# Index keys gathered by depth, without transposes, and a buffer of their own for block B's keys

## The chip, the cores and the metric

The kernel runs on one core of a Trainium2 chip. The metric is the device time of one execution in microseconds (us), as the median of several runs. A profiled execution gives the rows below.

## The reference

One step of a hybrid layer: RMSNorm, one combined input projection, sparse attention beside a gated short convolution, and an output projection. 1024 prompt rows and 8 sequences of 4 new tokens each go through it.

```python
p = split_proj(rmsnorm(x, norm_in) @ w_in)          # q, k, v, z_attn, q_idx, k_idx, w_idx, h, b, c, z_conv
...
dots = jnp.einsum("bthd,bld->bthl", qi, ki)          # 16 index heads of 64
s = jnp.einsum("bth,bthl->btl", wi, jax.nn.relu(dots))
_, idx = lax.top_k(s, 256)                           # the keys that attention may use
...
ki_past = cache_kidx[page_table].reshape(Bd, past, IDX_DIM)   # decode: 8 x 8192 cached index keys of 64
...
return x + mix @ w_out
```

## The kernel before, in words

The activations are kept transposed, as 16 chunks of 128 columns of the model width, each as a high and a low part (`xh`, `xl`). A weight tile is loaded as 128x4x128 (`w`, SyncE's queue), split by ScalarE into a high part `wh` and by VectorE into a low part `wl` (`load_w`, L485), and TensorE multiplies three products of the parts into `pj` (`proj`, L498). `wh` and `wl` have three buffers each, so a tile's `wl` can't be written before TensorE has read the one three tiles earlier. The weight tiles are numbered here in the order in which TensorE meets them, from 1; a tile of block B is 12 `pj` matmuls of 512 columns.

Block A is the first 512 prompt rows with the 32 decode rows, block B the other 512 prompt rows. After every tile `slot()` lets four pipes go on by a unit: index scores and attention of the prompt, the decode sequences' scores, selection and attention, and others. All of it is in one program, and the order on each engine is fixed when the program is built; an engine runs its rows strictly in that order.

The decode index is 64 units `keys(g, s)` (L1092), one for each group of 1024 cached keys of a sequence. A unit gathers 128 rows of 2 KB with one indirect DMA issued by GpSimd (`G`, L1096), transposes the four 128x128 pieces on TensorE into PSUM (`gt`, L174), splits them into `gkh` (ScalarE) and `gkl` (VectorE), and multiplies (`gd`, `da`); sums go into `S`, 128x2304. When all are in, `decode_find` (L1166) looks for the threshold of every query's 256 best keys with some forty passes over `S` on VectorE, then `way` (L1239), the page of each chosen key (`pt`, `pg`, `ids`, `rid`), and only then are `Ks` and `Vs` gathered.

Meanwhile block B's projections go on. The index key of block B is projected, normalised on VectorE (`kiv`, `kir`, `kit`: `ki_rest`, L565) and transposed on TensorE (`kip`). Then the heads: a key's raw projection is transposed (`kraw` into `p`), its root mean square found on VectorE (`kv`, `kr`), it is scaled and rotated on GpSimd (L656 to L551), and transposed back (`kp`) into `kt1` (`k_rest`, L647). `kt1` lies in the buffer that `S` had, and `head_tiles` (L712) calls `slot()` until the selection is done (`dsel`) before it takes it.

Of the kernel before, what the change touches and what calls it, by code (L numbers as in the profile page):

```python
# [60 lines left out]
def constants():  # L61
    res, dec = Cst(), Cst()
    res.add("ident", np.eye(128))
    r = np.arange(128)
    res.add("tri", np.concatenate([np.zeros((128, 128)), np.where(r[None, :] <= r[:, None], 0.0, NEG)], 1))
    pos_dec = 8192 + np.arange(32) % 4
    rope = np.zeros((128, 9, 48), np.float32)
    for gi in range(9):
        if gi == 4:
            pos = np.concatenate([np.arange(96), pos_dec])  # L70
        else:
            pos = np.arange(128) + 128 * (gi if gi < 4 else gi - 1)
        c, s = _angles(pos, 16)
        rope[:, gi, 0:16], rope[:, gi, 16:32] = c, s
        c, s = _angles(pos, 8)
        rope[:, gi, 32:40], rope[:, gi, 40:48] = c, s
    res.add("rope", rope.reshape(128, -1))
    c, s = _angles(pos_dec, 16)
    res.add("roped", np.concatenate([c, s], 1))
    q = np.arange(32)  # L80
    res.add("newm", np.where(np.arange(4)[None, :] <= (q % 4)[:, None], 0.0, SENT))
    res.add("own", (q[:, None] // 4 == q[None, :] // 4))
    res.add("prow", (r % 16)[:, None])
    wm = np.zeros((128, 8, 2, 32), np.float32)
    for p in range(128):
        for s in range(8):
            wm[p, s, p // 64, s * 4 + (p % 64) // 16] = 1.0
    dec.add("sel8", (np.arange(8)[:, None] == r[None, :] // 16))
    e16 = np.zeros((32, 2, 128), np.float32)
    for qq in range(32):  # L90
        e16[qq, qq // 16, (qq % 16) * 8:(qq % 16) * 8 + 8] = 1.0
    dec.add("e16", e16.reshape(32, -1))
    same = r[:, None] % 32 == r[None, :] % 32
    dec.add("msum", same)
    dec.add("mlow", same & (r[:, None] < r[None, :]))
    selk, selv = np.zeros((128, 132)), np.zeros((128, 2, 32))
    for p in range(128):
        selk[p, p // 8 * 8 + 4 + p % 4] = 1.0
        selv[p, p // 8 % 2, p // 16 * 4 + p % 4] = 1.0
    dec.add("selk", selk)  # L100
    dec.add("selv", selv.reshape(128, -1))
    dec.add("iota", np.broadcast_to(np.arange(256) - 256, (128, 256)))
    dec.add("wmask", wm.reshape(128, -1))
    cq = np.zeros((2, 128, 800), np.float32)
    tok = np.concatenate([np.arange(256, 512), pos_dec, np.arange(512, 1024)])
    c, s = _angles(tok, 8)
    cq[0] = 1.0
    for h in range(2):
        cq[0, h * 64:h * 64 + 8], cq[0, h * 64 + 8:h * 64 + 16] = c.T, c.T
        cq[1, h * 64:h * 64 + 8], cq[1, h * 64 + 8:h * 64 + 16] = -s.T, s.T  # L110
    return res, dec, cq


def build(tc, ctx, I, O, stop=None):
# [55 lines left out]
    def const(shape, name, dt=F32):  # L170
        return cp.tile(list(shape), dt, name=name, tag=name)
# [64 lines left out]
    def cs(name, rows=128):  # L236
        a, n = res.cols[name]
        return cst[:rows, a - 128:a - 128 + n]
# [50 lines left out]
    class Pipe:  # L289
# [11 lines left out]
        def slot(self):  # L301
            self.turn += 1
            if self.turn * 4 % self.every >= 4:
                return
            for u in list(self.active):
                if next(u, None) is None:
                    self.active.remove(u)
            while self.src and len(self.active) < self.depth:
                u = next(self.src[0], None)
                if u is None:  # L310
                    self.src.pop(0)
                    continue
                if u is not waiting and next(u, None) is not None:
                    self.active.append(u)
                break
# [169 lines left out]
    def load_w(view, eng=None):  # L485

        m = view.shape[-1]
        with first() if eng is None else nullcontext():
            w = wp.tile([128, 4, 128], F32, tag="w", bufs=4, name="w")
            lo = wp.tile([128, 4, 128], F32R, tag="wl", bufs=3, name="wl")  # L490
            hi = wp.tile([128, 4, 128], F32R, tag="wh", bufs=3, name="wh")
            w, lo, hi = w[:, :, :m], lo[:, :, :m], hi[:, :, :m]
            nc.sync.dma_start(w, view)
            nc.scalar.copy(hi, w)  # L494
            (tt if eng is None else eng.tensor_tensor)(lo, w, hi, SUB)
        return hi, lo
# [214 lines left out]

    def head_tiles(b, x):  # L712
        if b == 1:
            while "dsel" not in done:
                slot()
            kt1 = gp.tile([128, 2, 2, 512], F32R, tag="sc", bufs=1, name="kt1")
            kth[1], ktl[1] = kt1[:, 0], kt1[:, 1]
        for kv in range(2):
            follow(k_rest(b, kv, proj1(w_in, C_K + 128 * kv, 128, x, HALVES[b])))
            slot()  # L720
        for kv in range(2):
            follow(v_rest(b, kv, proj1(w_in, C_V + 128 * kv, 128, x, HALVES[b])))
            slot()
        for h in range(8):
            follow(q_rest(b, h, proj1(w_in, C_Q + 128 * h, 128, x, HALVES[b])))
            slot()
        follow(q_norm(b))
# [308 lines left out]
    def decode_index():  # L1036
        while not {"qi0", "ki0"} <= done:
            yield waiting
        st, acc = {}, {}
        cki = I["cache_kidx"].rearrange("o n (r e) d -> (o n r) (e d)", e=8)  # L1040
        zq = lambda z, s: z[:, s].rearrange("p r t h -> p (r t h)")
        keep = dec_c.cols["iota"][0]
        dc = const((128, keep), "dc")
        dcs = lambda k, r=128: dc[:r, dec_c.cols[k][0]:dec_c.cols[k][0] + dec_c.cols[k][1]]
        idx = const((128, 64), "gidx", I32)
        sc["msum"], sc["mlow"] = dcs("msum"), dcs("mlow")
        sc["e16"] = dcs("e16", 32).rearrange("q (g p) -> q g p", g=2)
        sc["selk"], sc["selv"] = dcs("selk"), dcs("selv").rearrange("p (k c) -> p k c", k=2)

        def tables():  # L1050
            nc.sync.dma_start(dc, I["dcst"][:, :keep])
            pt8i, pt8 = sm((8, 64), I32, name="pt8i"), sm((8, 64), name="pt8")
            nc.sync.dma_start(pt8i.rearrange("j (s g) -> j s g", s=8), I["page_table"].rearrange("s (g j) -> j s g", j=8))
            nc.vector.tensor_copy(pt8, pt8i)
            pp8 = psb((128, 64), name="pp8")
            nc.tensor.matmul(pp8, dcs("sel8", 8), pt8, start=True, stop=True)
            ts(idx, pp8, 16.0, cs("prow"), MUL, ADD)
            st["idx"] = idx
            yield 1

# [31 lines left out]
        def keys(g, s):  # L1092
            while "idx" not in st:
                yield 1
            G = g2((128, 512), name="G")
            nc.gpsimd.indirect_dma_start(out=G, out_offset=None, in_=cki,  # L1096
                                         in_offset=bass.IndirectOffsetOnAxis(ap=idx[:, 8 * s + g:8 * s + g + 1], axis=0))
            yield 1
            yield 1
            pt = psb((128, 512), name="gt")  # L1100
            for e in range(4):
                transpose(pt[:, 128 * e:128 * e + 128], G[:, 128 * e:128 * e + 128])
            kh, kl = g2((128, 512), F32R, name="gkh"), g2((128, 512), F32R, name="gkl")
            nc.scalar.copy(kh, pt)
            tt(kl, pt, kh, SUB)
            yield 1
            while "z" not in st:
                yield 1
            zh, zl, ws = st["z"]
            ps = psb(name="gd")  # L1110
            mm3(ps, zq(zh, s), zq(zl, s), kh, kl)
            rh, rl = g2((128, 512), F32R, name="rh"), g2((128, 512), F32R, name="rl")
            nc.scalar.activation(out=rh, in_=ps, func=AF.Relu)
            stt(rl, ps, 0.0, rh, ALU.max, SUB)
            yield 1
            if s == 0:
                acc[0] = psb((128, 512), name="da")
            nc.tensor.matmul(acc[0], ws[:, s], rh, start=s == 0, stop=False)
            nc.tensor.matmul(acc[0], ws[:, s], rl, start=False, stop=s == 7)
            if s == 7:  # L1120
                c = g // 2
                tmp = g2((64, 512), name="stmp")
                nc.scalar.copy(tmp, acc[0][64:128])
                dst = sc["S"][32 * c:32 * c + 32, (g % 2) * 1024:(g % 2) * 1024 + 1024].rearrange(
                    "q (p e r) -> q r e p", e=4, r=2)
                for r in range(2):
                    rs = slice(32 * r, 32 * r + 32)
                    tt(dst[:, r], acc[0][rs].rearrange("q (e p) -> q e p", e=4),
                       tmp[rs].rearrange("q (e p) -> q e p", e=4), ADD)
# [489 lines left out]
```

## Time and profile before

| | |
|---|---|
| median of 3 runs | 2208.34 us (2207.94 to 2208.93) |
| the profiled execution | 2209.53 us, of which its span is 2207.6 us |
| TensorE busy | 2162.5 us, 98% of the span |
| VectorE busy | 1317.3 us, 60% |
| ScalarE busy | 1088.3 us, 49% |
| GpSimd busy | 480.5 us, 22% |
| mean granted TensorE clock | 0.995 of full speed |

Busy times are sums over the whole span: an engine with 60% may be full for a hundred microseconds. `PEld` is TensorE's weight load, which overlaps its matmuls. A matmul's listed time is longer than the step from one to the next, since they are pipelined.

### The profile page before, as it was taken

How to read it: one execution, taken by the hardware profiler on the slowest of the kernel's cores; microseconds unless marked ns; L12 is line 12 of the kernel's file. 1: busy time of each engine (PE TensorE's matmuls, PEld its weight loads, DVE VectorE, ACT ScalarE, POOL GpSimd, SP SyncE). 2: the span in 40 equal slices, each digit the busy share in tenths (PEclk: the TensorE clock that was granted, in tenths of full speed). 3: DMA queues.
4: the chain of work that ended last, by engine and by line, in shares of the span. 5: the costliest groups of instructions: out<-in, count | busy, mean ns of one | idle time of the engine just before them, and what ended most of it. 6: DMA issues, size and time to landing. Idle time of an engine off the chain costs nothing.

```text
span 2207.6 us, 37829 instructions
## 1 busy us (share of the span) xinstructions
PE 2162.5 (98%) x13502; PEld 1941.8 (88%) x13502; DVE 1317.3 (60%) x2994; ACT 1088.3 (49%) x2112; POOL 480.5 (22%) x697
## 2 busy tenths in 40 slices
PE   6999999999999999999899999999999999999999
PEld 5899999999999999787688888888888899999887
DVE  6556666555555654799866666556667556443222
ACT  4346666334436566422257684445675565332221
POOL 2111011111113222142531143432331111210000
PEclk9999999999999999999999999999999999999999
DMA  5423444344344333333343344433343384448343
GB/s 195 131 90 117 125 138 135 118 141 131 123 144 140 118 116 104 107 117 113 102 134 117 117 150 129 118 122 105 113 128 113 102 301 117 123 119 275 134 134 110
DMA packets 203720, 290.81 MB, mean 132 GB/s; under 512 B 37588, under 2 KB 87948, under 8 KB 203404
## 3 DMA queue, kind: packets, MB, share of 16 engines
q1 hardware_dynamic: 192268, 254.83, 36.0%
q0 software_dynamic: 11264, 33.57, 5.5%
q8 instruction: 106, 1.74, 0.3%
q14 instruction: 82, 0.67, 0.1%
HBM read 247.53 MB, written 40.78 MB: 131 GB/s over the span
## 4 chain that ended last, share of the span: by engine, by line
PE 50%; DMA 0%; DVE 0%; issue 0%; POOL 0%
PE pj L512 33%; PE po L1503 8%; PE ix L855 1%; PE ix L854 1%; PE pt L174 1%; PE lg L1346 1%; PE dpo L1412 1%; PE kst L174 1%; PE sc L178 1%; PE sc L179 1%; PE po L179 1%; PE po L177 1%; PE po L178 1%; PE sc L177 1%; PE p L174 0%; PE pq L174 0%
## 5 line engine op out<-in xcount | busy, mean ns | idle before, releaser
L512 PE MATMUL pj<-xh,wl 128*128 128x288 f32 (+2 forms) x2800 | 793.0, 329 | 6.9 <-DVE wl L121 6.8
L512 PE MATMUL pj<-xh,wh 128*128 128x288 f32 (+2 forms) x2800 | 791.1, 328 | 6.9 <-DVE xl L121 2.7
L512 PE MATMUL pj<-xl,wh 128*128 128x288 f32 (+2 forms) x2800 | 796.1, 330 | 0.0
L121 DVE TENSOR_TENSOR wl<-w,wh 128x512 fp32r<-128x512 f32 (+1 forms) x613 | 444.1, 726 | 431.2 <-ACT wh L494 397.2
L494 ACT CAST wh<-w 128x512 fp32r<-128x512 f32 x616 | 379.2, 616 | 604.8 <-PE pj L512 380.0
L512 PEld LDWEIGHTS pj<-xh,wh 128*128 128x128 f32 (+1 forms) x2800 | 477.1, 189 | 51.8 <-DVE xl L121 3.1
L512 PEld LDWEIGHTS pj<-xh,wl 128*128 128x128 f32 (+1 forms) x2800 | 474.6, 189 | 51.6 <-DVE wl L121 11.2
L512 PEld LDWEIGHTS pj<-xl,wh 128*128 128x128 f32 (+1 forms) x2800 | 475.1, 189 | 42.2
L886 ACT ACTIVATE junk<-acc,se,se 128x512 int8<-128x512 f32 (+5 forms) x186 | 181.1, 974 | 27.4 <-DVE se L121 24.2
L1096 POOL DMA_INDIRECT G<-in_cache_kidx,gidx x64 | 64.3, 1004 | 388.6 <-PE gd L179 140.4
L121 DVE SCALAR_TENSOR_TENSOR acc<-ixr,wsg,acc 128x512 f32<-128x512 f32 (+3 forms) x150 | 98.3, 668 | 45.9 <-ACT ixr L857 44.7
L857 ACT ACTIVATE ixr<-ix,wab 128x512 f32<-128x512 f32 (+3 forms) x160 | 95.3, 613 | 54.9 <-PE ix L855 53.6
L512 PE MATMUL pj<-mxh,wl 128*128 128x272 f32 x512 | 109.8, 292 | 0.0
L512 PE MATMUL pj<-mxl,wh 128*128 128x272 f32 x512 | 109.4, 291 | 0.0
L512 PE MATMUL pj<-mxh,wh 128*128 128x272 f32 x512 | 108.9, 291 | 0.0
L1392 POOL DMA_INDIRECT Vs<-in_cache_v,rid x64 | 66.4, 1038 | 123.8 <-DVE Vl L121 36.1
L1004 ACT CAST pthl<-pt 128x256 fp32r<-128x256 f32 x144 | 49.6, 371 | 80.6 <-PE pt L174 79.4
L121 DVE TENSOR_TENSOR pthl<-pt,pthl 128x256 fp32r<-128x256 f32 x144 | 57.2, 420 | 50.6 <-ACT pthl L1004 50.0
L512 PEld LDWEIGHTS pj<-mxh,wh 128*128 128x128 f32 x512 | 81.5, 189 | 0.7
L512 PEld LDWEIGHTS pj<-mxl,wh 128*128 128x128 f32 x512 | 81.6, 189 | 0.3
L512 PEld LDWEIGHTS pj<-mxh,wl 128*128 128x128 f32 x512 | 81.3, 189 | 0.4
L990 POOL TENSOR_SCALAR P<-P,l 128x128 f32<-128x128 f32 (+7 forms) x64 | 51.9, 811 | 133.5 <-DVE l L989 102.7
(430 smaller groups left out, 3233.7 us busy)
## 6 DMA issues: line engine op xcount, KB each, us to landing
w<-in_w_in SPq DMA_DIRECT2D x480, 256.0 KB
w<-in_w_out SPq DMA_DIRECT2D x128, 256.0 KB
q_d<-qt SPq DMA_DIRECT2D x72, 64.0 KB
xr<-in_x_a SPq DMA_DIRECT2D x16, 272.0 KB
out_y_a<-xr SPq DMA_DIRECT2D x16, 272.0 KB
xq<-in_x_prompt SPq DMA_DIRECT2D x8, 512.0 KB
xq<-in_x_prompt SPq DMA_DIRECT2D x16, 256.0 KB
q<-q_d SPq DMA_DIRECT2D x32, 128.0 KB
```

What stands on the lines that cost most here:

```text
L121: i = f(*a, **k)
L174: nc.tensor.transpose(out, in_, ident[:p, :p])
L177: nc.tensor.matmul(out, lh, rh, start=start, stop=False)
L494: nc.scalar.copy(hi, w)
L512: nc.tensor.matmul(p[:m, :n], w[c][:, k % 4], x[k][b][:, a:a + n], start=(k == 0 and c == b), stop=(k == KT - 1 and c == 1))
L857: nc.scalar.activation(out=r[:, :w], in_=ps[:, :w], func=AF.Relu, scale=wab[:, g, h:h + 1])
L886: nc.scalar.activation(out=junk[:, :n], in_=S, func=AF.Sign, scale=sg, bias=cand, accum_out=s)
L990: nc.gpsimd.tensor_scalar(P[:, :n], P[:, :n], l, 0.5, MUL, MUL)
L1004: nc.scalar.copy(t[:, 0], ptv)
L1096: nc.gpsimd.indirect_dma_start(out=G, out_offset=None, in_=cki, in_offset=bass.IndirectOffsetOnAxis(ap=idx[:, 8 * s + g:8 * s + g + 1], ax ...
L1392: nc.gpsimd.indirect_dma_start(out=W[:, hf], out_offset=None, in_=cv, in_offset=bass.IndirectOffsetOnAxis(ap=rid[:, hf, q:q + 1], axis=0))
L1503: nc.tensor.matmul(ps[i], x[k_][b][:, 128 * i:128 * i + 128], w[c], start=(k_ == 0 and c == b), stop=(k_ == KT - 1 and c == 1))
```

## The change

The index keys of the cache come transposed from the host (page, depth, token). A unit gathers with four indirect DMAs of 128 rows of 512 B, so that each 128x128 piece arrives with depth on the partitions; the four transposes, their PSUM tile and the rows of `gt` are gone, and `gkh` and `gkl` are made from `G` itself. The table of row numbers holds four entries for a unit, and `S` has its columns in another order. `kt1` is a tile of its own, and the loop that waited for `dsel` is gone. `wl` and `wh` get a fourth buffer each, and the memory for indirect DMA descriptors is cut from 16384 to 2048 bytes a partition.

```diff
-            lo = wp.tile([128, 4, 128], F32R, tag="wl", bufs=3, name="wl")
-            hi = wp.tile([128, 4, 128], F32R, tag="wh", bufs=3, name="wh")
+            lo = wp.tile([128, 4, 128], F32R, tag="wl", bufs=4, name="wl")
+            hi = wp.tile([128, 4, 128], F32R, tag="wh", bufs=4, name="wh")
...
         if b == 1:
-            while "dsel" not in done:
-                slot()
-            kt1 = gp.tile([128, 2, 2, 512], F32R, tag="sc", bufs=1, name="kt1")
+            kt1 = const((128, 2, 2, 512), "kt1", F32R)
...
-        cki = I["cache_kidx"].rearrange("o n (r e) d -> (o n r) (e d)", e=8)
+        cki = I["cache_kidx"].rearrange("n d t -> (n d) t")
...
-            G = g2((128, 512), name="G")
-            nc.gpsimd.indirect_dma_start(out=G, out_offset=None, in_=cki,
-                                         in_offset=bass.IndirectOffsetOnAxis(ap=idx[:, 8 * s + g:8 * s + g + 1], axis=0))
-            yield 1
-            yield 1
-            pt = psb((128, 512), name="gt")
+            G = g2((128, 4, 128), name="G")
             for e in range(4):
-                transpose(pt[:, 128 * e:128 * e + 128], G[:, 128 * e:128 * e + 128])
+                nc.gpsimd.indirect_dma_start(out=G[:, e], out_offset=None, in_=cki,
+                                             in_offset=bass.IndirectOffsetOnAxis(ap=idx[:, s, g, e:e + 1], axis=0))
+            yield 1
+            yield 1
+            G = G.rearrange("p e t -> p (e t)")
             kh, kl = g2((128, 512), F32R, name="gkh"), g2((128, 512), F32R, name="gkl")
-            nc.scalar.copy(kh, pt)
-            tt(kl, pt, kh, SUB)
+            nc.scalar.copy(kh, G)
+            tt(kl, G, kh, SUB)
...
-    nc = _bacc.Bacc("TRN2", target_bir_lowering=False, num_devices=1)
+    nc = _bacc.Bacc("TRN2", target_bir_lowering=False, num_devices=1, dynamic_dma_scratch_size=2048)
...
+    host["cache_kidx"] = np.ascontiguousarray(host["cache_kidx"][0].transpose(0, 2, 1))
```

The two programs stand in different orders on TensorE and VectorE. On TensorE before, `kip` (the transposes of block B's index key) stands in the middle of weight tile 286:

```order
L512 MATMUL pj<-xl,wh 128x512
L512 MATMUL pj<-xh,wl 128x512
L512 MATMUL pj<-xh,wh 128x512
L174 MATMUL kip<-ident,kit 128x128 x4
L512 MATMUL pj<-xl,wh 128x512
L512 MATMUL pj<-xh,wl 128x512
L512 MATMUL pj<-xh,wh 128x512
```

In the changed program the same transposes stand between weight tiles 292 and 293, behind the last rows of block A's attention (`pt`, `po`), and the first key's `p` right behind them:

```order
L179 MATMUL po<-pthl,vl_102 128x256
L174 MATMUL pt<-ident,P 128x128 x2
L177 MATMUL po<-pthl,vh_101 128x256
L178 MATMUL po<-pthl,vh_101 128x256
L179 MATMUL po<-pthl,vl_102 128x256
L177 MATMUL po<-pthl,vh_101 128x256
L178 MATMUL po<-pthl,vh_101 128x256
L179 MATMUL po<-pthl,vl_102 128x256
L174 MATMUL kip<-ident,kit 128x128 x4
L174 MATMUL p_13201<-ident,kraw 128x128 x4
L512 MATMUL pj<-xh,wh 128x512
L512 MATMUL pj<-xl,wh 128x512
```

Behind these come the 48 `pj` of tiles 293 to 296, then the first `kp` and the second `p`; tiles 297 and 298, the first row of 299, `pidx` and `pqd`, eight more rows of 299, and the second `kp` follow. So 108 `pj` of tiles 284 to 292 and the attention's 24 `po`, 16 `pt` and 6 `sc` lie between the end of tile 283 and `kip`.

On VectorE before, around the copy that ends the index key's normalisation (`kit<-kit`), at most two passes over `S` stand between two `wl`:

```order
L121 TENSOR_TENSOR wl<-w,wh 128x512
L121 TENSOR_TENSOR S<-S 128x2304
L550 TENSOR_TENSOR kit<-ro_12406,ro_12407 128x4x8
L551 TENSOR_TENSOR kit<-ro_12408,ro_12409 128x4x8
L121 TENSOR_TENSOR S<-S 128x2304
L121 TENSOR_TENSOR wl<-w,wh 128x512
L592 COPY kit<-kit 128x4x64
L121 TENSOR_TENSOR S<-S 128x2272
L121 TENSOR_TENSOR wl<-w,wh 128x512
L121 TENSOR_SCALAR S<-S 128x2304 x2
```

In the changed program the last of these rows are:

```order
L121 TENSOR_TENSOR S<-S 128x2304
L121 TENSOR_TENSOR wl<-w,wh 128x512
L121 TENSOR_SCALAR kiv<-kiv 128x4
L121 TENSOR_SCALAR S<-S 128x2304
L121 TENSOR_TENSOR pthl<-pt,pthl 128x256 x2
L121 TENSOR_SCALAR kirh<-kiv 128x4
L121 TENSOR_SCALAR S<-S 128x2304
L121 TENSOR_SCALAR kir<-kirh 128x4
L121 TENSOR_TENSOR S<-S 128x2304
L121 TENSOR_TENSOR kirt<-kir 128x4
L121 TENSOR_TENSOR pthl<-pt,pthl 128x256 x2
L121 TENSOR_TENSOR S<-S 128x2304
```

The `wl` at the top is that of weight tile 296, and the next `wl` comes 24 passes over `S` later. Between it and the copy that ends `kit` stand 16 passes over `S` (9 TENSOR_TENSOR, 7 TENSOR_SCALAR), 4 `pthl`, 1 `zt` and 20 small rows of the normalisation. Ahead of it, from the `wl` of tile 287 on, stand 9 `wl`, 19 passes over `S` (9 TENSOR_TENSOR and 6 TENSOR_SCALAR of 2304, 4 of 1024), 4 `pthl` and 12 shorter rows, softmax's for the most part. Behind the copy, up to the last `kr` of the first key, stand 6 TENSOR_TENSOR and 3 TENSOR_SCALAR over `S`, `way`, 4 `wl`, the first `pt` and `pg`, and the small rows of `kv` and `kr`; then 27 `pt` and the second key's small rows up to its last `kr`.

On GpSimd, the gathers stand in one piece, in both programs, between the rows of block A's heads; before:

```order
L1075 MEMSET zqh 64x8x64
L1075 MEMSET zql 64x8x64
L1096 DMA G<-in_cache_kidx,gidx 128x512 x64
L958 TENSOR_TENSOR q_7520<-q_7520,ssq 128x256
L959 TENSOR_TENSOR q_7520<-q_7520,gq 128x256
```

In the changed program:

```order
L1073 MEMSET zqh 64x8x64
L1073 MEMSET zql 64x8x64
L1095 DMA G<-in_cache_kidx,gidx 128x128 x256
L956 TENSOR_TENSOR q_7392<-q_7392,ssq 128x256
L957 TENSOR_TENSOR q_7392<-q_7392,gq 128x256
```

No other row of GpSimd's lies between two gathers. On TensorE the 64 units were spread over 86 weight tiles, and are spread over 102 now.

## Rows read from the trace of the kernel before

**Rows 1.** The page: busy us, share of the span and instructions of each engine.
```profile
PE 2162.5 (98%) x13502; PEld 1941.8 (88%) x13502; DVE 1317.3 (60%) x2994; ACT 1088.3 (49%) x2112; POOL 480.5 (22%) x697
```

**Rows 2.** Window: length, then busy us (instructions) by engine, clock, DMA share, GB/s.
```profile
550.00:600.00 50.00, 50.00 (x370) 47.60 (x369) 25.63 (x47) 19.45 (x37) 9.28 (x9) 1.00 0.38 120
```

**Rows 3.** Windows of 50 us from 850 to 1150 us, with the sum of all six.
```profile
900.00:950.00 50.00, 48.46 (x235) 38.35 (x236) 40.46 (x80) 17.55 (x37) 18.26 (x25) 0.97 0.30 96
...
1050.00:1100.00 50.00, 39.12 (x170) 30.27 (x169) 41.50 (x90) 11.64 (x21) 26.36 (x30) 0.90 0.30 94
...
sum 300.00, PE 282.29 PEld 234.12 DVE 241.78 ACT 119.93 POOL 106.85; mean PE 47.05 PEld 39.02 DVE 40.30 ACT 19.99 POOL 17.81
```

**Rows 4.** Timeline of TensorE at the first kp: start, length, row, idle before.
```profile
1076.92 0.69 PE L174 MATMUL kp<-ident,kt 128*128 128x128 f32 x4 [1.83 <-POOL kt L551]
...
1083.64 0.80 PE L512 MATMUL pj<-xh,wh 128*128 128x512 f32 x1 [1.96 <-ACT vraw L644]
```

**Rows 5.** Timeline of TensorE around one unit's transposes.
```profile
553.25 0.60 PE L174 MATMUL gt<-ident,G 128*128 128x128 f32 x4
553.61 0.37 PE L512 MATMUL pj<-xl,wh 128*128 128x256 f32 x1
553.82 0.41 PE L512 MATMUL pj<-xh,wl 128*128 128x288 f32 x2
```

**Rows 6.** Transposes and gathers by tile: count, min/median/max ns; landing by line.
```profile
L174 PE MATMUL gt<-ident,G x256: 269/272/273, 277.9 to 637.3; 128*128 128x128 f32 x128
L1096 POOL DMA_INDIRECT G<-in_cache_kidx,gidx x64: 944/945/1433, 266.7 to 625.8; - x64
...
DMA to landing us min/median/max: 3.2/3.6/6.6
```

**Rows 7.** Timeline of GpSimd: one gather of index keys, then key gathers back to back.
```profile
542.15 0.94 POOL L1096 DMA_INDIRECT G<-in_cache_kidx,gidx  x1 [4.47 <-PE gd L179]
...
1096.74 0.94 POOL L1321 DMA_INDIRECT Ks<-in_cache_k,rid  x1 [0.30 <-issue]
1097.99 0.95 POOL L1321 DMA_INDIRECT Ks<-in_cache_k,rid  x1 [0.30 <-issue]
```

**Rows 8.** Windows of 5 us near the start.
```profile
55.00:60.00 5.00, 2.77 (x19) 2.33 (x19) 2.50 (x5) 2.33 (x5) 0.60 (x1) 1.00 0.46 151
60.00:65.00 5.00, 3.75 (x16) 2.99 (x16) 4.55 (x10) 0.98 (x3) 0.00 (x0) 0.52 0.25 79
```

**Rows 9.** Timeline of VectorE: single rows of the selection and around it.
```profile
975.72 1.51 DVE L121 TENSOR_SCALAR S<-S 128x1024 int16<-128x1024 int16 x1
977.15 0.68 DVE L121 TENSOR_TENSOR wl<-w,wh 128x512 fp32r<-128x512 f32 x1
977.75 0.75 DVE L121 TENSOR_SCALAR S<-S 128x2304 int16<-128x2304 int16 x1
978.42 0.41 DVE L121 TENSOR_TENSOR pthl<-pt,pthl 128x256 fp32r<-128x256 f32 x1
...
979.75 1.35 DVE L121 TENSOR_TENSOR S<-S 128x2304 int16<-128x2304 int16 x1
...
1061.71 4.23 DVE L1239 TENSOR_REDUCE way<-S 128x256 f32<-128x2304 int16 x1
...
1071.22 0.29 DVE L121 TENSOR_TENSOR pt<-pt,pt 128x256 int16<-128x256 int16 x1
...
1071.55 0.35 DVE L121 TENSOR_SCALAR pt<-pg,ptc 128x256 int16<-128x256 int32 x1
```

**Rows 10.** Timeline of GpSimd: first and last row of the first key's rotation.
```profile
1071.67 1.14 POOL L656 TENSOR_TENSOR kt<-kt,kr 128x512 f32<-128x512 f32 x1 [10.50 <-DVE kr L121]
...
1076.50 0.36 POOL L551 TENSOR_TENSOR kt<-ro,ro 128x64 f32<-128x64 f32 x1
```

**Rows 11.** What TensorE waited for from 850 to 1110 us: total, times, longest.
```profile
PE pj L512 <- DVE wl L121: 5.3, 5, 1.7
...
PE pt L174 <- POOL P L990: 2.2, 2, 1.8
```

More of the change, by code (lines that the diff above doesn't have):

```diff
@@ L82, in constants @@
     res.add("own", (q[:, None] // 4 == q[None, :] // 4))
-    res.add("prow", (r % 16)[:, None])
+    res.add("prow", (r % 64)[:, None])
     wm = np.zeros((128, 8, 2, 32), np.float32)
@@ L87, in constants @@
             wm[p, s, p // 64, s * 4 + (p % 64) // 16] = 1.0
-    dec.add("sel8", (np.arange(8)[:, None] == r[None, :] // 16))
+    dec.add("sel2", (np.arange(2)[:, None] == r[None, :] // 64))
     e16 = np.zeros((32, 2, 128), np.float32)
@@ L1044, in decode_index @@
         dcs = lambda k, r=128: dc[:r, dec_c.cols[k][0]:dec_c.cols[k][0] + dec_c.cols[k][1]]
-        idx = const((128, 64), "gidx", I32)
+        idx = const((128, 8, 8, 4), "gidx", I32)
         sc["msum"], sc["mlow"] = dcs("msum"), dcs("mlow")
@@ L1051, in tables @@
             nc.sync.dma_start(dc, I["dcst"][:, :keep])
[L1052 to L1057, printed above, removed]
+            pt2i, pt2 = g2((2, 256), I32, name="pt2i"), g2((2, 256), name="pt2")
+            nc.sync.dma_start(pt2i.rearrange("r (s c) -> r s c", s=8), I["page_table"].rearrange("s (c r) -> r s c", r=2))
+            nc.vector.tensor_copy(pt2, pt2i)
+            pp2 = psb((128, 256), name="pp2")
+            nc.tensor.matmul(pp2, dcs("sel2", 2), pt2, start=True, stop=True)
+            ts(idx.rearrange("p s g e -> p (s g e)"), pp2, 64.0, cs("prow"), MUL, ADD)
             st["idx"] = idx
@@ L1094, in keys @@
                 yield 1
-            G = g2((128, 512), name="G")
-            nc.gpsimd.indirect_dma_start(out=G, out_offset=None, in_=cki,
-                                         in_offset=bass.IndirectOffsetOnAxis(ap=idx[:, 8 * s + g:8 * s + g + 1], axis=0))
+            G = g2((128, 4, 128), name="G")
+            for e in range(4):
+                nc.gpsimd.indirect_dma_start(out=G[:, e], out_offset=None, in_=cki,
+                                             in_offset=bass.IndirectOffsetOnAxis(ap=idx[:, s, g, e:e + 1], axis=0))
             yield 1
             yield 1
-            pt = psb((128, 512), name="gt")
-            for e in range(4):
-                transpose(pt[:, 128 * e:128 * e + 128], G[:, 128 * e:128 * e + 128])
+            G = G.rearrange("p e t -> p (e t)")
             kh, kl = g2((128, 512), F32R, name="gkh"), g2((128, 512), F32R, name="gkl")
-            nc.scalar.copy(kh, pt)
-            tt(kl, pt, kh, SUB)
+            nc.scalar.copy(kh, G)
+            tt(kl, G, kh, SUB)
             yield 1
@@ L1124, in keys @@
                 dst = sc["S"][32 * c:32 * c + 32, (g % 2) * 1024:(g % 2) * 1024 + 1024].rearrange(
-                    "q (p e r) -> q r e p", e=4, r=2)
+                    "q (e r p) -> q r e p", e=4, r=2)
                 for r in range(2):
```

## The prediction

> **What bounds the kernel now.** I began with the page: TensorE is busy for 98% of the span, every other engine for 60% or less [rows 1]. So what leaves TensorE's list comes off the time, unless TensorE waits for it elsewhere. Two stretches matter. Where the index keys are gathered, TensorE has no idle time at all: 50.00 of 50 us, VectorE at half, GpSimd at a fifth [rows 2]. Around the selection, 850 to 1150 us, it is otherwise: TensorE is busy for 282.3 of 300 us, so 17.7 us are idle, and VectorE is full for much of it (241.8 of the 300 us) [rows 3]. The clock stood at 0.97 and 0.90 in two of these windows, half speed for part of each, behind a wait both times; at half speed half the work is lost, so the shares missing cost 1.5 and 5 us. **The stretch loses 24.2 us in all.** The waits are for `wl` (5.3 us), `P`, `kp`, `vraw` and their like [rows 4, 11]: rows of VectorE that stand behind passes over `S`. The reader should keep both: 28 us to win in the first stretch, and a second in which VectorE's list, not TensorE's, sets the pace.
>
> **The change, part by part.**
>
> *The transposes.* Four `gt` start at 553.25 us and the next `pj` at 553.61, which then takes 0.21 us to the following one, where its like takes about 0.13 (370 matmuls in 50 us [rows 2]) [rows 5]. That is 0.36 + 0.08 = 0.44 us a unit, and 64 units make **28.1 us**. TensorE is full there, so all of it counts. Bounds: 64 x 0.36 = 23 us below; above, the 256 listed lengths of 0.272 us over two, 35 us, for they overlap [rows 6].
>
> *Four gathers for one.* A gather holds GpSimd for 0.945 us [rows 6], and the next begins 1.25 us after it [rows 7]: four take 5.0 us a unit. A unit comes every (625.8 - 266.7) / 63 = 5.70 us now [rows 6], of which GpSimd waits 4.5 us [rows 7]. By the order given above, 64 units are spread over 102 weight tiles in place of 86; 16 tiles of 24 matmuls at 0.135 us are 52 us, so a unit comes every 5.70 - 0.44 + 0.81 = 6.07 us. GpSimd keeps ahead by 1 us a unit, and I cost it at nothing. If every gather took the longest seen, 1.433 + 0.305 us, a unit would need 6.95 us and 64 units 56 us more. Landing takes 3.6 us [rows 6]; the fourth lands 5.0 + 3.6 us after the first issue, with two units' time to be used.
>
> The trace shows that gathers overlap, one starting every 1.25 us though each lands after 3.2 us at the earliest [rows 6, 7]. The Trainium skill, "DMA: Bandwidth & Descriptors", section "Anatomy of one DMA — SWDGE (gpsimd) path", gives each DMA a fixed cost of about 2.0 us and adds bytes over 436 GB/s; four of 64 KB one behind the other would by that be about 8.6 us a unit (an estimate from that page), over the 6.07, and the sum would grow by some 160 us. The trace speaks against this reading.
>
> The smaller descriptor memory is not shown by any row. Below, it costs nothing; above, each gather would wait until its predecessor has landed, 4 x 3.6 = 14.4 us a unit, 64 x (14.4 - 6.07) = 533 us. Five or so gathers in flight are few, so I take nothing.
>
> *The other edits.* `gkh` and `gkl` read SBUF for PSUM: same count, on engines half idle there. The table is one more small step at the start. The removed loop never turns: counted over the calls of `slot()`, the selection is done at the 257th, and block B's heads begin at the 280th, in both programs. `kt1` in the buffer of `S` waited for `way`, which ended at 1065.9 us [rows 9]; `kp`, ahead of the first write to `kt1`, ran at 1076.9 [rows 4]. So the heads did not wait for the selection, and this part is worth nothing by itself.
>
> *A fourth buffer for `wl` and `wh`.* In the stretch from 55 to 65 us TensorE is idle 3.5 us and runs 5 us at 0.52 of full clock: 5.9 us lost [rows 8]. A deeper buffer may take none of it or all; I take **3 us**.
>
> *The order around the selection.* Here it costs. The units are further apart, so the selection stands later among the weight tiles, and its tail falls into block B's index key and heads. Take as time 0 the end of tile 283 on TensorE. The `wl` of tile 287 needs the buffer that tile 283 leaves, so on VectorE nothing behind it can start before. From there to the copy that ends `kit`, by the counts above:
> - 18 TENSOR_TENSOR of `S` at 1.35, 13 TENSOR_SCALAR at 0.75, 4 of 1024 at 1.51: 40.1 us [rows 9]
> - 9 `wl` at 0.68 and 8 `pthl` at 0.41: 9.4 us [rows 9]
> - 12 short rows, 20 of the normalisation, `zt` and the copy: some 8.3 us, by the lengths of such rows there.
>
> That is 57.8 us. Before's own rows from 979.75 us to `way` at 1061.71 (82.0 us [rows 9]) give 78.3 by the same lengths, since some are stretched while GpSimd works; so I add 4.7%: 60.5 us. With 0.7 for the `wl`, `kip` can start at 61.3. TensorE has until then 108 `pj` at 0.2325 us, 24 `po`, 16 `pt` and 6 `sc`: 31.1 us (a 512-column step is 0.2325 in the trace, a 256-column one 0.12, a transpose 0.11). It stands still for **30 us**: everything behind `kip` on its queue waits, and all the following projections are behind it. In the order before, a `wl` comes after two passes at most, so TensorE waited for 5.3 us of `wl` in all [rows 11]; here none comes in 24 passes.
>
> Next, `kp`. Rows up to the first key's `kr`: 6 + 3 passes, `way` (4.23), 4 `wl`, the first `pt` and small ones, 24.3 us, 25.4 with the 4.7%. GpSimd's rotation takes 1071.67 to 1076.86, 5.2 us [rows 10]. So `kp` can start at 61.2 + 25.4 + 5.2 = 91.8. TensorE has `kip`, `p` and 48 `pj`, 12.1 us, and is done at 73.4: **18 us** idle. If it runs at half clock behind the first wait, that is hidden in the second. Then 27 `pt` at 0.29 and 0.35 us [rows 9] and the second key's rows take until 101.5, GpSimd until 106.8; TensorE gets to the second `kp` at 101.8: **5 us**, and 0.7 for the `p` between.
>
> These make 54.3 us. What remains of before's: `P` and the low clock behind it (2.2 + 1.5), `vraw` (2.0) and about 1 us of half clock at the end [rows 3, 4, 11]. Together 61 us against 24.2: **37 us more**. Below: rows can follow each other 0.08 us closer than their length (the pass at 977.75 us, 0.67 us before the next [rows 9]); with that for all 86 rows ahead of `kip` and no stretching, the first wait is 20 us, the second 14, the whole some 45, 21 more than before. Above: twice the stretching, 9.4%, makes 6 us more up to the second `kp`, and another 4 where GpSimd's own rows would be stretched likewise.
>
> **The sum**, against the profiled execution's own 2209.5 us (1.2 over the median): 2209.5 - 28.1 - 3 + 37 = 2215.4; as a median 2214.2. I say **2214 us**.
>
> **The rivals.** 2212.8 us and more is slower, 2203.9 and less faster: 0.2% is what a measurement of this kernel can tell.
> 1. *The waits are smaller* (faster). The place is `kip`: if VectorE's list up to `kit` takes under about 48 us from the end of tile 283, TensorE waits 17 and not 30, all waits come to about 41, and the time is 2209.5 - 28.1 - 3 + 17 - 1.2 = 2194. If there are no more waits than before, 2177. For it: the 0.08 us steps. Against: 82.0 us measured where the listed lengths give 78.3.
> 2. *A draw*: waits of 51 to 59 us leave 2204 to 2212.
> 3. *GpSimd becomes the bound* in the gathers: at 6.95 us a unit 56 us more, 2270; with each gather waiting for the landing of the one before, 533 more, 2747. For it: a gather of 1.433 us is in the trace. Against: the median is its least, 0.945, and key gathers overlap [rows 6, 7].
>
>    (By the Trainium skill's page and section named above, with gathers in single file, the estimate is some 160 us more than the forecast, a chance of 0.01 within this rival's.)
>
> 4. *The heads start earlier* since the loop is gone: would show as more gain; the loop never turned, so I give it no chance of its own.
>
> **How the numbers follow.** The forecast (waits of 59 to 72 us) 0.50, rival 1 0.20, rival 2 0.24, rival 3 0.06. The range reaches into rival 1 at 2195 and up to 2227, the forecast with the stretched passes and no gain at the start; its own range, given that it comes, is 2211 to 2227. Slower 0.54 (0.48 of the forecast, its part above 2212.8, and rival 3), same 0.26, faster 0.20.
>
> **What would show it.** Right: no `gt`; TensorE full between 270 and 630 us; a wait before `kip` of 20 us or more, put down to VectorE's `kit`, then one before `kp`, put down to GpSimd; low clock behind both; a gap of some 35 us between two `wl`. Wrong: GpSimd full in the gathers and TensorE idle before `gd` (rival 3), or a wait before `kip` under 15 us (rival 1). The start would show by windows from 55 to 65 us without idle time.

## The result, and the profile after

The changed kernel takes **2240.21 us** (median of four runs, 2234.61 to 2244.2), the kernel before 2208.64 beside it: a ratio of 1.014 (1.0117 to 1.0163). The forecast was 2214, range 2195 to 2227. The sign was right, the size was not: 31.6 us slower, where 6 were foreseen.

One execution of `e2_scratch_alone`, a kernel below, took 4312 us, where its other nine took 2205 to 2213; it is not in that kernel's ratio.

The profiled execution is the fastest of the four, 2234.61 us with a span of 2232.8, so what follows explains 25.2 us of span; the 5.6 us up to the median are in no trace. First the page: busy us by engine (it answers to [rows 1]), and the group of the gathers with its count, busy us, mean ns, and the idle time ahead of it.

```profile
PE 2144.2 (96%) x13246; PEld 1919.1 (86%) x13246; DVE 1299.9 (58%) x2994; ACT 1083.9 (49%) x2112; POOL 680.6 (30%) x889
...
L1095 POOL DMA_INDIRECT G<-in_cache_kidx,gidx x256 | 261.4, 1021 | 245.2 <-ACT qsq L637 96.4
```

TensorE has 256 matmuls less and 18 us less busy time, in a span that is 25 us longer: the loss is idle time and slow clock, not work. The windows of the changed kernel say where (columns as in [rows 2, 3]):

```profile
250.00:300.00 50.00, 40.20 (x271) 37.13 (x270) 25.89 (x70) 24.59 (x53) 20.50 (x21) 0.86 0.41 114
500.00:550.00 50.00, 48.24 (x340) 44.95 (x339) 23.95 (x44) 17.28 (x34) 32.87 (x32) 1.00 0.43 133
550.00:600.00 50.00, 49.16 (x356) 46.87 (x355) 26.03 (x49) 20.00 (x40) 33.58 (x32) 1.00 0.38 120
1050.00:1100.00 50.00, 19.95 (x74) 15.24 (x74) 49.71 (x85) 5.94 (x12) 16.50 (x14) 0.65 0.14 43
1100.00:1150.00 50.00, 42.30 (x206) 34.09 (x207) 30.15 (x76) 18.97 (x39) 26.59 (x38) 0.87 0.39 117
...
270.00:275.00 5.00, 3.01 (x22) 2.62 (x20) 1.63 (x4) 2.99 (x7) 3.78 (x5) 1.00 0.42 124
275.00:280.00 5.00, 0.91 (x3) 0.66 (x3) 0.50 (x3) 0.21 (x2) 3.78 (x5) 0.68 0.28 85
280.00:285.00 5.00, 1.61 (x5) 0.84 (x5) 0.00 (x0) 0.00 (x0) 2.83 (x3) 0.50 0.18 52
285.00:290.00 5.00, 4.67 (x17) 3.99 (x17) 1.77 (x3) 3.22 (x7) 0.00 (x0) 0.50 0.24 65
```

Two stretches are hurt. The one at 1050 us was foreseen: VectorE is full (49.71 of 50 us) and TensorE busy for 19.95. The other is where the gathers run, in which TensorE had no idle time before [rows 2]. It is worst from some 10 us after the first gather on: three matmuls in 5 us, with ScalarE and VectorE nearly still and the DMA engines busy for 0.18 to 0.28 of the time. GpSimd is not full where the gathers run (33 of 50 us, from 500 to 600 us).

The waits of TensorE (us in total, times, longest) in the gathers' stretch (250 to 700 us), and behind the dots around the selection (850 to 1200 us):

```profile
PE pj L512 <- issue: 12.2, 20, 1.9
PE p L174 <- issue: 3.6, 3, 1.5
PE da L1115 <- ACT rh L1110: 1.0, 1, 1.0
...
PE kip L174 <- DVE kit L592: 15.6, 1, 15.6
PE kp L174 <- POOL kt L551: 9.9, 1, 9.9
PE pj L512 <- ACT kraw L644: 3.5, 1, 3.5
PE pt L174 <- DVE kiv L121: 2.6, 1, 2.6
PE p L174 <- DVE kt L121: 2.2, 1, 2.2
```

"issue" is idle time for which the profile shows nothing that was waited for. To add idle time and slow clock in one measure, I took from each trace, for every TensorE matmul, the step to the next one's start less the median step of its form, and summed this excess by stretch; the rest is the work itself:

| us | before | after | difference | predicted |
|---|---|---|---|---|
| work at median steps | 2141.6 | 2114.3 | -27.3 | -28.1 |
| lost, 0 to 100 us | 25.2 | 19.1 | -6.1 | -3 |
| lost, 250 to 700 us (gathers) | -1.6 | 29.0 | **+30.6** | **0** |
| lost, 850 to 1200 us (selection) | 26.2 | 55.4 | +29.2 | +37 |
| lost elsewhere | 1.6 | 1.3 | -0.3 | 0 |

The differences make +26.1, the spans differ by 25.2.

What GpSimd did while TensorE stood still: GpSimd's timeline, then TensorE's (start, us, and in brackets the idle time before).

```profile
263.23 1.22 POOL L1095 DMA_INDIRECT G<-in_cache_kidx,gidx  x1 [96.36 <-ACT qsq L637]
...
272.36 0.94 POOL L1095 DMA_INDIRECT G<-in_cache_kidx,gidx  x1 [0.30 <-issue]
273.61 0.94 POOL L1095 DMA_INDIRECT G<-in_cache_kidx,gidx  x1 [0.30 <-issue]
...
282.50 0.94 POOL L1095 DMA_INDIRECT G<-in_cache_kidx,gidx  x1 [0.30 <-issue]
293.93 1.45 POOL L1095 DMA_INDIRECT G<-in_cache_kidx,gidx  x1 [10.49 <-DVE ssq L639]
```

```profile
272.35 0.29 PE L512 MATMUL pj<-xh,wh 128*128 128x288 f32 x1
273.41 0.28 PE L512 MATMUL pj<-xh,wh 128*128 128x256 f32 x1 [0.77 <-issue]
274.85 0.29 PE L512 MATMUL pj<-xl,wh 128*128 128x288 f32 x1 [1.16 <-issue]
276.99 0.37 PE L512 MATMUL pj<-xl,wh 128*128 128x256 f32 x1 [1.85 <-issue]
279.08 0.40 PE L512 MATMUL pj<-xh,wl 128*128 128x288 f32 x1 [1.72 <-issue]
280.51 0.37 PE L174 MATMUL p<-ident,qraw 128*128 128x128 f32 x1 [1.03 <-issue]
...
284.00 0.37 PE L174 MATMUL p<-ident,qraw 128*128 128x128 f32 x1 [1.50 <-issue]
284.72 0.57 PE L512 MATMUL pj<-xh,wl 128*128 128x256 f32 x1 [0.34 <-issue]
...
1071.41 1.12 PE L174 MATMUL kip<-ident,kit 128*128 128x128 f32 x4 [15.60 <-DVE kit L592]
...
1101.68 1.12 PE L174 MATMUL kp<-ident,kt 128*128 128x128 f32 x4 [9.89 <-POOL kt L551]
```

`G` takes its buffers from ten that other tiles of the kernel share (`g2`), so GpSimd can issue the gathers of several units in one go: at the start those of four units, sixteen, one every 1.25 us or a little more. The first eight cost TensorE nothing. From about the ninth to 2 us after the last its matmuls come singly, 1.4 or 2.1 us apart, and they are `pj` and `p`, which need no index key. Counting gathers less than 1.9 us apart as one row, and TensorE's loss until 5 us after its last, the trace has 25 rows of 4 (-0.3 us lost in all), 16 of 8 (13.3 us) and one each of 12 (1.0) and 16 (13.3). So it is not the number of gathers alone that hurts, but their standing in a row. How tight the row is matters as well as its length: the one row of eight in which no step is over 1.26 us (at 346.80 us) cost 4.5 us, the fifteen others, each with a step of 1.4 us or more somewhere, 8.8 us together.

### The profile page after: what moved, and what is told of

The parts are those of the page before. It is cut to its first block, busy times and chain, and to the rows that moved or that the text cites. A ratio compares the mean times of both kernels' runs of the same rounds, so it can differ in the third digit from the quotient of the medians.

```text
span 2232.8 us, 37661 instructions
## 1 busy us (share of the span) xinstructions
PE 2144.2 (96%) x13246; PEld 1919.1 (86%) x13246; DVE 1299.9 (58%) x2994; ACT 1083.9 (49%) x2112; POOL 680.6 (30%) x889
## 4 chain that ended last, share of the span: by engine, by line
PE 50%; DMA 0%; ACT 0%; issue 0%; DVE 0%; POOL 0%; ACTq 0%
PE pj L512 32%; PE po L1500 8%; PE ix L853 1%; PE ix L852 1%; PE pt L174 1%; PE lg L1343 1%; PE dpo L1409 1%; PE kst L174 1%; PE sc L178 1%; PE sc L179 1%; PE po L179 1%; PE po L178 1%; PE po L177 1%; PE sc L177 1%; PE p L174 0%; PE pq L174 0%
## 5 line engine op out<-in xcount | busy, mean ns | idle before, releaser
L1095 POOL DMA_INDIRECT G<-in_cache_kidx,gidx x256 | 261.4, 1021 | 245.2 <-ACT qsq L637 96.4
L956 POOL TENSOR_TENSOR q<-q,ssq 128x256 f32<-128x256 f32 x32 | 22.2, 694 | 241.1 <-DMA q<-q_d 145.8
L1015 POOL TENSOR_TENSOR zt<-zt 128x256 fp32r<-128x256 f32 x32 | 25.7, 803 | 191.5 <-ACT zt L1014 170.1
```

The source lines that it names most:

```text
L1095: nc.gpsimd.indirect_dma_start(out=G[:, e], out_offset=None, in_=cki, in_offset=bass.IndirectOffsetOnAxis(ap=idx[:, s, g, e:e + 1], axis=0))
```

## The experiments

Losses in the table are counted as above, in us, by stretch; ratios are to the kernel before, timed on the same chip.

| kernel | median us | ratio (95%) | 0-100 | 250-700 | 850-1200 | from 1200 |
|---|---|---|---|---|---|---|
| e1_gathers_alone | 2239.76 | 1.0135 (1.0118-1.0152) | 21.2 | 29.9 | 57.3 | 1.4 |
| e4_gathers_small | 2240.49 | 1.0146 (1.0129-1.0163) | 22.1 | 30.1 | 54.6 | 1.5 |
| e2_scratch_alone | 2210.15 | 1.0003 (0.9993-1.0013) | 21.4 | -1.4 | 29.9 | 1.7 |
| e3_bufs_alone | 2204.39 | 0.9977 (0.9967-0.9988) | 19.7 | -1.7 | 25.2 | 1.1 |
| g6_one_buffer | 2359.48 | 1.0683 (1.0665-1.0701) | 21.7 | 66.3 | 86.2 | 25.9 |
| s2_hold | 2277.64 | 1.0311 (1.0293-1.0328) | 21.1 | 33.8 | 14.8 | 83.0 |
| c1_hold_single_gather | 2263.90 | 1.0255 (1.0238-1.0272) | 19.8 | -1.4 | 10.0 | 81.2 |
| h1_pause | 2249.48 | 1.0176 (1.0156-1.0196) | 25.9 | 35.2 | 55.2 | 1.4 |
| c3_hold_index_key | 2223.33 | 1.0054 (1.0035-1.0073) | 25.4 | -1.3 | 24.4 | 22.4 |
| h2_pause_memsets | 2232.13 | 1.0109 (1.0091-1.0127) | 19.3 | 23.5 | 57.5 | 1.5 |
| k2_four_large | 2343.94 | 1.0612 (1.0589-1.0635) | 21.9 | 120.5 | 28.3 | 12.5 |
| h3_pause_short | 2231.05 | 1.0091 (1.0074-1.0108) | 21.5 | 25.3 | 55.3 | 1.4 |

**Which part of the change costs.** Four kernels take the change apart.

`e1_gathers_alone`: the gathers and the layout of the index keys only (the edit is shown against the changed kernel; `wh` goes like `wl`).

```diff
-            lo = wp.tile([128, 4, 128], F32R, tag="wl", bufs=4, name="wl")
+            lo = wp.tile([128, 4, 128], F32R, tag="wl", bufs=3, name="wl")
...
-            kt1 = const((128, 2, 2, 512), "kt1", F32R)
+            while "dsel" not in done:
+                slot()
+            kt1 = gp.tile([128, 2, 2, 512], F32R, tag="sc", bufs=1, name="kt1")
...
-    nc = _bacc.Bacc("TRN2", target_bir_lowering=False, num_devices=1, dynamic_dma_scratch_size=2048)
+    nc = _bacc.Bacc("TRN2", target_bir_lowering=False, num_devices=1)
```

> The transposed gathers alone: three buffers for wl and wh, kt1 in the buffer of S with its loop, 16384 bytes of descriptor memory, all as before. Its order on TensorE is that of the changed kernel. If the small descriptor memory starves TensorE in the gathers, TensorE loses under 5 us between 250 and 700 us here (the changed kernel loses 29 there), and the time is about 2215. If the 256 gathers themselves do it, some 25 to 30 us are lost there and the time is about 2238 (the changed kernel's, and the 6 us of the start not won). The theory that the order costs in the selection expects about 55 us lost from 850 to 1150 us either way.

The gathers alone give the whole result, both losses and the time; its waits around the selection are the changed kernel's:

```profile
PE kip L174 <- DVE kit L592: 15.6, 1, 15.6
PE kp L174 <- POOL kt L551: 9.4, 1, 9.4
```

The other edits (the separate `kt1`, the removed loop, the fourth buffers, the descriptor memory) add nothing that can be seen when taken together, 2239.8 against 2240.2 us; `kt1` and the loop were not tried by themselves.

`e4_gathers_small`: the same with the small descriptor memory (`dynamic_dma_scratch_size=2048`).

> As the kernel with the gathers alone, but with 2048 bytes of descriptor memory. Descriptor memory as the cause: 25 to 30 us lost between 250 and 700 us, some 25 us slower than the kernel with 16384 bytes. The gathers as the cause: as the kernel with 16384 bytes, within 5 us.

`e2_scratch_alone`: the kernel before with the small descriptor memory.

> The kernel before with 2048 bytes of descriptor memory and nothing else changed; its order is that of before. Descriptor memory as the cause: 64 gathers of 2 KB rows, one at a time, may lose a little (0 to 8 us), and the 64 key gathers back to back some more. The gathers as the cause: 2208, no change.

Neither moves. The descriptor memory is out as a cause of the issue waits: they are there with 16384 bytes as with 2048.

`e3_bufs_alone`: the kernel before with `bufs=4` for `wl` and `wh`; the descriptor memory is 12288, to make room.

> The kernel before with four buffers for wl and wh, and 12288 bytes of descriptor memory to make room. If the fourth buffer is what took 6 us out of the first 100 us, that shows here: 2202, with TensorE losing 19 us of the first 100 in place of 25. If not, 2208. In the selection, kip stands at weight tile 284 in place of 286, and wl can be further ahead: 0 to 5 us less lost there.

This is faster than both kernels, by 0.23% of the one before. Its profile has 5.5 us less lost in the first 100 us than the profile of before, but e1 and e2, with three buffers, have 4 us less too: of the 4.7 us in the median, the profile can place little at the start for certain.

**Is it the row of gathers?** `g6_one_buffer` is the changed kernel with one buffer for `G`, so that a unit's gathers wait until the unit before is split.

```diff
-            G = g2((128, 4, 128), name="G")
+            G = gp.tile([128, 4, 128], F32, tag="gg", bufs=1, name="G")
```

> The changed kernel, but G has one buffer of its own, so GpSimd never issues more than the four gathers of a unit in one go. If TensorE starves because many gathers follow each other without a pause, the 15 us lost between 250 and 300 us (16 gathers in one go there) fall under 4, and the rest of the stretch loses the same or less: about 2225 us. If the number of gathers decides, whatever their spacing, some 28 us are lost over the stretch of the units as before: about 2240. The selection stands still later here (way at weight tile 300 in place of 297, 35 passes between two wl), so that its loss is not smaller than the changed kernel's 56 us.

The time was missed by far (about 2225 us expected, 2359 measured), but the trace decides. The only wait of TensorE listed from 250 to 700 us:

```profile
PE gd L177 <- ACT gkh L1101: 51.9, 40, 3.0
```

With rows of four and a pause of some 4 us (3.1 to 5.7) between them, no "issue" wait is left. What costs now is that a unit comes only every 8.9 us, since the gathers, their landing and the split follow one another; the units last until 824 us, so part of their cost lies behind the stretch of the table. The clock is 0.97 of full or more in every 50 us of the units. So the number of gathers is not enough to make the idle time.

`k2_four_large` asks whether their size is: the kernel before, transposes kept, with three more gathers per unit of the same 2 KB rows, into tiles that nothing reads.

```diff
+            for j in range(3):
+                spare_ = gp.tile([128, 512], F32, tag=f"sp{j}", bufs=2, name=f"X{j}")
+                nc.gpsimd.indirect_dma_start(out=spare_, out_offset=None, in_=cki,
+                                             in_offset=bass.IndirectOffsetOnAxis(ap=idx[:, 8 * s + g:8 * s + g + 1], axis=0))
```

> The kernel before with three more gathers a unit of the same 128 rows of 2 KB, into tiles that nothing reads, and 2048 bytes of descriptor memory to make room for them: as many gathers in a row as in the changed kernel, but of rows of 2 KB, and with the transposes. If the unbroken row of gathers starves TensorE whatever their size, 20 to 30 us are lost from 250 to 700 us. If it is the rows of 512 B, under 5 us are lost there (ten key gathers of 1 KB rows in one go cost 1 to 3 us in the traces so far).

TensorE's waits from 250 to 700 us:

```profile
PE pj L512 <- issue: 47.6, 63, 2.9
PE da L1122 <- issue: 12.2, 7, 4.6
PE gd L177 <- issue: 5.1, 2, 4.6
PE gt L174 <- issue: 4.8, 6, 1.7
```

The same kind of idle time, four times as much (69.7 us in all against 16.2), in a kernel whose rows of gathers are longer (27 in a row from 263 us on), with rows of 2 KB. With half clock and the rest the loss is 120.5 us, where 20 to 30 were expected. Of the change this kernel has only the small descriptor memory, which cost nothing in `e2_scratch_alone` and `e4_gathers_small`. Rows of 512 bytes are not needed for the idle time. It moves four times the bytes of index keys, so by itself it can't tell the row from the bytes; but the changed kernel moves no more bytes than the one before, and has the idle time.

Three kernels put a pause between units. `h1_pause` writes an unused tile behind each unit's gathers (`nc.gpsimd.memset(pz, 0.0)`).

> The changed kernel with one more row on GpSimd: a memset of an unused 128x768 tile (0.8 us by the memsets of the trace before, so some 1.1 us between two units' gathers) behind the four gathers of every unit. The order on TensorE is that of the changed kernel. In its trace TensorE lost nothing in groups of four gathers, 0.8 us in each group of eight and 14.6 us in the one of sixteen. If an unbroken row of gathers is what starves TensorE, the loss between 250 and 700 us falls from 29 to under 6 us, and the time to about 2215 (up to 2222 if the pauses hold the units back). If it is the share of the time in which gathers run, the loss stays over 20 us.

The scheduler put the memsets ahead of all gathers, so there was no pause between units: it tells nothing of the question. `h2_pause_memsets` ties the pause to the unit: two memsets of `G` ahead of its gathers.

```diff
+            nc.gpsimd.memset(G, 0.0)
+            nc.gpsimd.memset(G, 0.0)
```

> The changed kernel with two memsets of G (128x512, some 0.5 us each) on GpSimd ahead of every unit's four gathers, which must wait for them, so that a pause of about 1 us stands between the gathers of two units (the memsets of the kernel with the unused tile were moved ahead of all gathers, and no pause came of them). TensorE's order is that of the changed kernel. If an unbroken row of more than four gathers starves TensorE, the loss from 250 to 700 us falls from 29 to under 8 us, and the time by some 20 us, less up to 10 where units of 6.1 to 6.3 us hold TensorE back. If a pause of GpSimd alone does not help, the 15 us lost in the first 16 gathers stay.

The rows are of four now, but for a first one of eight, with a pause of 1.4 us between them:

```profile
280.09 0.94 POOL L1097 DMA_INDIRECT G<-in_cache_kidx,gidx  x1 [0.30 <-issue]
281.03 0.55 POOL L1094 MEMSET G<- 128x512 f32 x1
281.64 0.57 POOL L1095 MEMSET G<- 128x512 f32 x1
282.48 0.95 POOL L1097 DMA_INDIRECT G<-in_cache_kidx,gidx  x1 [0.27 <-POOL G L1095]
```

From 250 to 300 us, where the changed kernel loses 14.6 us, this one loses -0.2. Its waits from 250 to 700 us:

```profile
PE gd L177 <- ACT gkh L1103: 13.5, 17, 2.5
PE gd L177 <- issue: 4.4, 5, 1.6
```

The issue waits fall from 16.2 to 4.4 us, and a wait for the keys takes their place, so that the loss is 23.5 us and not the 8 expected: with the pause a unit takes 6.4 us of GpSimd (four times 1.25, and 1.4), above the 6.07 at which TensorE wants them. `h3_pause_short` has one memset, some 0.8 us.

> As the kernel with two memsets of G ahead of every unit's gathers, with one: the pause between two units is 0.8 us in place of 1.4, and a unit takes GpSimd 5.9 us in place of 6.4, under the 6.07 us in which TensorE uses one. If the pause is enough to keep TensorE from starving, the loss from 250 to 700 us falls under 10 us (29 in the changed kernel, 23 with two memsets, of which 14 were waits for a unit's own gathers), and the time is about 2218. If a pause this short lets the gathers run into one row again, the idle time that nothing releases comes back: over 10 us of it, and 2230 or more.

TensorE's waits from 250 to 700 us:

```profile
PE pj L512 <- issue: 12.1, 20, 1.2
PE p L174 <- issue: 1.4, 2, 1.0
```

Units run into each other again (rows of 8, 12, 16 and 20), and issue waits of 14.1 us remain. The length of a row alone does not decide here either: the row of 16 at 266.74 us, 1.33 us from gather to gather on average, cost 12.4 us, and the row of 20 at 552.04 us, 1.45 us on average, 0.3. Where the limit lies between them, and whether it is the spacing or the place in the program, no run here tells. On this path a pause long enough to help is one that GpSimd can't afford: both kernels stay 20 us and more above the one before.

**Is the loss at the selection one of order?** `s2_hold` is the changed kernel with the passes over `S` held until block B's index key and both heads' keys are done.

```diff
+        while not {"ki1", "k10", "k11"} <= done:
+            yield 1
```

> The changed kernel, but the last part of the selection (the eight bit passes over S, way and what follows) is emitted only when block B's index key and its two keys are done. If the loss of 56 us around the selection is the order, passes over S between VectorE's steps for kit and kr, the waits before kip and kp fall from 16 and 10 us to under 5 each, the stretch from 850 to 1200 us loses under 25 us, and the time is about 2210. If the steps of kit and kr are slow by themselves, or the wl starve because of the held passes later, it stays over 2230.

`c1_hold_single_gather` is the same hold in a kernel with all of the change but the gathers.

> All of the change but the gathers (one gather of 2 KB rows and the four transposes a unit, as before), with the same hold on the selection's last part. If gathers and order are the two causes, TensorE loses nothing from 250 to 700 us and under 10 us around the selection in place of the 26 of before: with the 6 us of the start, 2183 to 2190, faster than both kernels. If the hold only moves the passes to where they starve wl again, 2200 to 2210.

`s2_hold` loses 14.8 us from 850 to 1200 us where the changed kernel loses 55.4, `c1_hold_single_gather` 10.0 where `e3_bufs_alone` loses 25.2, and no wait of `kip` or `kp` is left in either: the order makes that loss. The times were missed all the same (2210, and 2183 to 2190, were expected), for 81 to 83 us come back, nearly all at the end of block B. TensorE's waits in `s2_hold` from 1700 to 1950 us, where the kernel before had none:

```profile
PE pt L174 <- POOL P L988: 23.6, 12, 5.0
PE sc L177 <- DVE mx L980: 7.9, 3, 5.2
```

As I read the order, the prompt's selections and attention take turns with these passes, come later, and at the end have no projections left to hide behind; no run tests this reading by itself. `c3_hold_index_key` holds the passes for the index key alone (`ki1`), again without the gathers.

> All of the change but the gathers, and the bit passes of the selection are emitted only when block B's index key is done (not its head keys, as in the kernel that held them longer and lost 80 us at the end). On TensorE kip comes at weight tile 272, way at 299, and the decode rows are gathered 7 tiles later than in the changed kernel. If passes among the steps of kit are what costs, TensorE waits for nothing at kip, the stretch from 850 to 1200 us loses 10 to 18 us in place of 25, and the time is 2190 to 2198. If the passes only move into the wl of the tiles behind, 2204, as with the fourth buffer alone.

`kip` does not wait, `kp` does (3.5 us), 24.4 us are still lost from 850 to 1200 us, where 10 to 18 were expected, and 22.4 from 1200 us on. Each hold moves the passes, none finds a place for them; no version with both gains was found, and `e3_bufs_alone` is the best that ran.

## Why the prediction was wrong

**The step that failed** is "GpSimd keeps ahead by 1 us a unit, and I cost it at nothing". Its premise held: GpSimd has time left (33 of 50 us), keys are there (`gd` waits for them 0.5 us), a unit takes 5 us. But the step asked only whether the gathers come in time. A tight row of them holds up every matmul, also those that need no key, and GpSimd, being ahead, makes such rows by itself whenever buffers for `G` are free. The stretch cost 30.6 us. The prediction's row for gathers back to back was a pair [rows 7], from a row of 14 that cost 1.7 us, and it looked at them for GpSimd's time alone. Rival 3 had the place, the gathers, and not the mechanism: it named a full GpSimd and a wait before `gd`. Gathers in single file did not come, as foreseen: here too they start 1.25 us apart, where one landed after 3.2 us at the earliest [rows 6]. By the fixed cost in the Trainium skill, "DMA: Bandwidth & Descriptors", section "Anatomy of one DMA — SWDGE (gpsimd) path", single file would be some 2.15 us each (an estimate from that page); no run here shows that.

**That it came out slower, as forecast, is luck.** The forecast set 37 us of waits at the selection against 31 us of gains. The waits came to 29.2 us and the gains to 33.4: without the loss among the gathers, which was put at nothing, the forecast's own sum would have come out some 4 us under the kernel before, about 2204 us, in the region of rival 2, the draw.

**The transposes**: -28.1 predicted, -27.3 measured as work. Right.

**The order around the selection**: right in mechanism, 37 predicted, 29.2 measured. VectorE's timeline shows the list, with its `wl` of tile 296, the copy that ends `kit`, the next `wl`, and the first key's last `kr`:

```profile
1049.05 0.68 DVE L121 TENSOR_TENSOR wl<-w,wh 128x512 fp32r<-128x512 f32 x1
...
1071.07 0.28 DVE L592 COPY kit<-kit 128x256 f32<-128x256 f32 x1
...
1086.16 0.68 DVE L121 TENSOR_TENSOR wl<-w,wh 128x512 fp32r<-128x512 f32 x1
...
1096.82 0.15 DVE L121 SCALAR_TENSOR_TENSOR kr<-krt,kr 128x4 f32<-128x4 f32 x1
```

The gap between the two `wl` is 37.1 us ("some 35" was said). From the `wl` of tile 287, at 1018.84 us, to the copy it is 52.2 us, not 60.5: the rows follow each other 0.08 us closer than their lengths, and the 4.7% for GpSimd's share did not come. That was the lower bound of the step, and it should have been the value. TensorE reached the wait 6 us later than reckoned, some 37 us after tile 283 and not 31: 2.6 us went to a wait for `kiv`, and half clock began behind it, at 1051.6 us, already ahead of `kip`. So `kip` waited 15.6 us and not 30, between the 20 that were called right and the 15 that were called wrong. From `kip` to `kp` it took 30.3 us, where 30.5 were reckoned; the 18 us of idle time there came as 9.9 before `kp`, 5.1 ahead of `p` and `pj`, and half clock between. The 5 us before the second `kp` did not come.

**The start**: 3 predicted, 6.1 in the profile. The kernels with three buffers lost 21 to 25 us there and those with four 19 to 26, so this is not put down to the buffer.

**At nothing**: the descriptor memory, right by e2 and e4; `kt1` and the loop, right as far as e1 shows, which takes them out together with the fourth buffers and the memory.

For the profiled execution the errors are +30.6 (gathers), -7.8 (order), -3.1 (start) and +0.8 (transposes), 20.5 in all; it took 2234.6, and 2215.4 was forecast for it, 19.2 less.

## What to carry to other kernels

When one indirect gather is split into several, ask not only whether GpSimd keeps up but how long its rows of gathers get: an engine that runs ahead strings units together, and here rows of eight and more, with hardly a break, cost the engine that was full, while rows of four cost it nothing. Count them in the order and the buffers that free them, and look at the other engines' "issue" waits beside GpSimd's timeline, not at GpSimd's busy share. And when work is spread further apart, look up what lands beside what behind it: 28 us of transposes saved were lost again, 400 us later, on VectorE's list.

## What was not expected of the hardware

- Gathers in a tight row, 1.25 us apart, left TensorE, ScalarE and VectorE nearly still. In the row of 16 it begins 9 us after the first gather (273 against 263.23 us). In a row of eight at 346.80 us the matmuls keep their pace for 8 us, and the idle time comes at its end. The matmuls then came at multiples of about 0.7 us (1.44, 2.14, 2.09, 1.43 us between starts), and the weights' DMA queue moved nothing from 276 to 288 us.
- Half clock follows: 0.50 of full speed, 1.2 GHz. The clock of 0.68 from 275 to 280 us means that it began near 277 us, when TensorE had run only single matmuls since 273; it lasted until 290.
- Why it happens stays open. The Trainium skill, "Runtime: NRT & Kernel Launch", section "Instruction fetch mechanics", has each engine fetch its instructions by DMA in blocks of 16 KiB. The trace agrees on the size (queue q8: 104 packets, 1.70 MB, one for every 130 matmuls or so, so q8 is taken for TensorE's), but no such block was on the way: in the trace's records they came at 269.81 and 301.04 us and took 1.0 and 1.6 us. A late block of TensorE's own does not explain it. The other queue of instruction blocks, q14, brought none between 262 and 288.8 us; before, its blocks at this place came at 281.2 and 283.4 us, and TensorE lost nothing. What part late blocks of the other engines have, if any, is not tested.
- Nor is it known why `Ks` escapes: a row of ten such gathers cost 1.8 us in the changed kernel, and one of 14 cost 1.7 in the kernel before. Both have steps of 1.4 to 1.8 us in them, at most six in a row being tight.
